# A two-block transformer kernel on one core: weights, activations and position bias laid out on the host in the order of their fetches

## The chip, the core and the metric

The kernel runs on one core of a Trainium2 chip. A core has a matrix engine (TensorE, PE in the rows; its weight loads are shown apart as PEld), a vector engine (VectorE, DVE), an engine for activation functions (ScalarE, ACT), a general one (GpSimd, POOL) and SyncE (SP), which here only issues loads and stores. Sixteen DMA engines move data between the chip's main memory (HBM) and the on-chip buffers that the engines compute on. Every engine works through its own instructions in a fixed order and waits on semaphores for the others.

The metric is the device time of one execution in microseconds (us).

## What is computed

256 rows of 1,024 numbers (float32) pass through four attention layers and two large feed-forward parts. The reference, cut to its frame:

```
x = even_layer(x, ...)                    # 8 products of rms_norm(x) with w_in, two kinds of attention, w_out
x = odd_layer(x, ...)                     # windowed attention with sinks; chunked attention with a bias by position
h = rms_norm_2(x, attn_norm[0]);  x = x + dsa_mixer(h, ...)         # top-k chosen keys
h = rms_norm_2(x, mlp_norm[0]);   x = x + squared_relu_mlp(h, mlp_w_up[0], mlp_w_down[0])
h = rms_norm_2(x, attn_norm[1]);  x = x + mla_mixer(h, ...)         # low-rank queries, keys, values
h = rms_norm_2(x, mlp_norm[1]);   x = x + squared_relu_mlp(h, mlp_w_up[1], mlp_w_down[1])
return rms_norm_2(x, final_norm)
```

The bias by position of the second layer is one number for each head and each distance between query and key:

```
rel = iq[:, None] - ik[None, :]
ridx = jnp.clip(rel, -(CHUNK - 1), REL_MAX) + (CHUNK - 1)     # 64 - 1, 256
s = s + rel_table[:, ridx]                                    # rel_table: 8 heads x 320
```

## The kernel before

**Products.** Activations lie with features on the 128 partitions (`xT`, 8 tiles of 128 features by 256 tokens). Every float32 operand is split into two reduced-precision halves, high and low (`h`, `l` for activations, `wh`, `wl` for weights), and a product is the sum of three matmuls (high by high, low by high, high by low). `N.tokens` gives a product with tokens on the partitions (matmuls of line 185), `N.features` one with features on the partitions (line 216).

**Weights.** Each product with a matrix of 1,024 rows is fed in blocks of 1,024 numbers a partition, 512 KB, as a rule four row tiles by 256 columns. `fetch` (line 115) issues one DMA on SP's queue for a block, into one of four buffers `raw`. ScalarE then copies it to `wh` (line 161), which rounds it, and VectorE subtracts to get `wl` (line 162). 24 matmuls use a block, and then the next block's buffer is due. In HBM a block is 512 pieces of 1 KB: each partition gets four pieces, a row tile apart, at a pitch of one row of the matrix (4,104 numbers, 16,416 bytes, for `even_w_in`; 4,096 numbers for `mlp_w_up`). The very first block is fetched in two halves between the loads of `x`.

**Order.** A list of names for each layer (`ORDER0` to `ORDER3`) gives the order in which the program is written, and a scheduler then sets the order on each engine from priorities; the queues themselves are in order. In layer 0 the list's first parts are the products for queries and keys, the statistics of the layer's norm (`layer_stats`: column sums on TensorE at line 325, then some ten short VectorE instructions from line 343 on), the head norm (lines 421 to 434), and the turning of queries and keys by TensorE (`split_t`, `split_k`: line 386). `forget_log` (`BL`) fetches a narrow block of eight columns (`narrow`, tile `wn`, lines 125 to 128).

**Waits of the loads.** A fetch may start when the buffer it fills has been read by VectorE (the `wl` of four blocks earlier), and SP issues nothing else while it waits. The tables of linear position bias (`alibi`, line 741) go through SP's queue too; the buffers `bias` (three) serve both kinds of bias.

**Bias by position.** `rel_bias` (lines 963 to 973) builds, for each of eight heads, a 128 by 384 table: two fills of a masked corner by GpSimd and four DMAs on GpSimd's queue, each of which reads 64 partitions that start one number apart in the 320 numbers of the head. The table is then stored mirrored, and the softmax reads it backwards (`falling=True`, line 521).

## Time and profile before

| | |
|---|---|
| median of 3 runs | 879.75 us (879.03 to 883.26) |
| the profiled execution's own time | 882.59 us |
| its span, first to last instruction | 880.9 us |
| TensorE busy | 846.0 us (96% of the span) |
| VectorE, ScalarE, GpSimd busy | 670.3, 578.8, 52.0 us |
| loads on SP's queue | 129,696 packets, 134.20 MB, 55.0% of the DMA engines' time |

Where TensorE is busy, it computes; what a change can win is to be looked for where it is idle or runs at a lower clock. Of the span's 40 slices of 22 us, the page shows TensorE under 90% in six: the first two, the seventh (132 to 154 us), the twelfth (242 to 264 us), the 28th and the last. The DMA engines are busiest in the first six, seven tenths or more in five of them. The share of DMA time and the GB/s are to be read together: a high share at few GB/s means packets that take long.

### The profile page before, as it was taken

Reading aid. Unit: us, or ns where it says so; the run is one execution under the profiler, and the core shown is the slowest. Engines: PE = TensorE matmul, PEld = TensorE weight load, DVE = VectorE, ACT = ScalarE, POOL = GpSimd, SP = SyncE. Lnnn points to the kernel's source line nnn. Section 1 sums busy time; section 2 is a strip of 40 time slices with the busy share of each in tenths; the row PEclk is TensorE's granted clock in tenths of the full one; section 3 lists DMA queues with packets and bytes.
Section 4 is the critical chain, followed back from the end, with each engine's and each line's share of the span. In section 5 each row is a group of like instructions: output and inputs, shape, how many; then the busy total and the mean of one; then the engine's idle time right before and its main releaser. Section 6 shows DMA issues by size and latency. Waiting matters only on the chain. (4 is left out here: it accounts for less than half of the span.)

```text
span 880.9 us, 17702 instructions
## 1 busy us (share of the span) xinstructions
PE 846.0 (96%) x6554; PEld 813.6 (92%) x6554; DVE 670.3 (76%) x1799; ACT 578.8 (66%) x1379; POOL 52.0 (6%) x130
## 2 busy tenths in 40 slices
PE   6899997999989999999999999998999999999996
PEld 6799987999989999899999999998999998889986
DVE  5879986789888879988765577668999966556654
ACT  5597974669787666987664466555997765446542
POOL 8100000002330100000000000002000000000000
PEclk9899998999999999999999999999999999999999
DMA  8979595554655652335655666553324665566751
GB/s 211 175 156 169 92 82 174 177 174 119 178 129 168 181 145 73 122 116 170 185 184 185 190 189 194 185 164 98 124 73 123 201 188 173 187 182 191 215 169 48
DMA packets 131430, 137.83 MB, mean 156 GB/s; under 512 B 8289, under 2 KB 123121, under 8 KB 131345
## 3 DMA queue, kind: packets, MB, share of 16 engines
q1 hardware_dynamic: 129696, 134.20, 55.0%
q0 software_dynamic: 1360, 1.99, 1.5%
q8 instruction: 51, 0.84, 0.4%
q10 hardware_dynamic: 288, 0.52, 0.2%
q14 instruction: 35, 0.28, 0.1%
HBM read 135.65 MB, written 1.05 MB: 155 GB/s over the span
## 5 line engine op out<-in xcount | busy, mean ns | idle before, releaser
L161 ACT ACTIVATE wh<-raw 128x512 fp32r<-128x512 f32 (+2 forms) x548 | 290.3, 571 | 221.3 <-issue 102.1
L162 DVE TENSOR_TENSOR wl<-raw,wh 128x512 fp32r<-128x512 f32 (+2 forms) x548 | 322.7, 620 | 126.7 <-ACT wh L161 119.9
L216 PE MATMUL mm<-ar,wh 128*128 128x256 f32 (+1 forms) x1664 | 304.8, 283 | 0.5 <-ACT ar L701 0.4
L216 PEld LDWEIGHTS mm<-ar,wh 128*128 128x128 f32 (+1 forms) x1664 | 258.0, 190 | 2.0 <-ACT ar L701 1.3
L185 PE MATMUL mm<-wh,ar 128*128 128x256 f32 (+2 forms) x1168 | 238.3, 299 | 9.0 <-ACT wh L161 7.5
L216 PE MATMUL mm<-ar,wl 128*128 128x256 f32 x832 | 234.4, 283 | 0.0
L185 PEld LDWEIGHTS mm<-wh,ar 128*128 128x128 f32 x1168 | 188.5, 192 | 14.5 <-ACT wh L161 7.8
L185 PE MATMUL mm<-wl,ar 128*128 128x256 f32 (+2 forms) x584 | 174.1, 299 | 1.1 <-DVE wl L162 1.1
L216 PEld LDWEIGHTS mm<-ar,wl 128*128 128x128 f32 x832 | 157.5, 190 | 0.4 <-DVE wl L162 0.2
L185 PEld LDWEIGHTS mm<-wl,ar 128*128 128x128 f32 x584 | 111.7, 191 | 4.4 <-DVE wl L162 2.0
L216 PE MATMUL s<-ar,wh 128*128 128x256 f32 x512 | 90.4, 279 | 0.0
L216 PEld LDWEIGHTS s<-ar,wh 128*128 128x128 f32 x512 | 78.0, 188 | 0.0
L216 PE MATMUL s<-ar,wl 128*128 128x256 f32 x256 | 71.4, 279 | 0.0
L524 ACT ACTIVATE se<-sx,mx 128x128 f32<-128x128 f32 (+1 forms) x128 | 57.1, 451 | 4.9 <-DVE mx L521 4.3
L216 PEld LDWEIGHTS s<-ar,wl 128*128 128x128 f32 x256 | 48.1, 188 | 0.0
L216 PE MATMUL pv<-ar,wh 128*128 128x256 f32 x256 | 45.1, 279 | 0.0
L216 PEld LDWEIGHTS pv<-ar,wh 128*128 128x128 f32 x256 | 39.0, 188 | 0.0
L216 PE MATMUL pv<-ar,wl 128*128 128x256 f32 x128 | 35.7, 279 | 0.0
L544 DVE TENSOR_TENSOR pt<-tp,pt 128x384 fp32r<-128x384 f32 x60 | 32.2, 552 | 3.4 <-ACT pt L543 2.9
L493 PE MATMUL s<-kbh,ar 128*128 128x512 f32 (+1 forms) x112 | 31.2, 354 | 0.8 <-ACT kbh L397 0.7
L543 ACT ACTIVATE pt<-tp 128x384 fp32r<-128x384 f32 x60 | 27.9, 486 | 1.1 <-PE tp L542 0.7
L1213 ACT ACTIVATE ar<-u 128x512 fp32r<-128x512 f32 x32 | 20.3, 633 | 11.8 <-DVE u L1211 11.7
(309 smaller groups left out, 1157.9 us busy)
## 6 DMA issues: line engine op xcount, KB each, us to landing
raw<-in_mlp_w_up SPq DMA_DIRECT2D x64, 512.0 KB, 3.8
raw<-in_mlp_w_down SPq DMA_DIRECT2D x64, 512.0 KB, 4.0
raw<-in_even_w_in SPq DMA_DIRECT2D x31, 512.0 KB, 9.1
raw<-in_odd_w_in SPq DMA_DIRECT2D x26, 512.0 KB, 4.7
raw<-in_a_w_in SPq DMA_DIRECT2D x16, 512.0 KB, 3.7
raw<-in_even_w_out SPq DMA_DIRECT2D x8, 512.0 KB, 4.6
raw<-in_odd_w_out SPq DMA_DIRECT2D x8, 512.0 KB, 3.4
raw<-in_a_w_out SPq DMA_DIRECT2D x8, 512.0 KB, 3.6
```

The lines of the kernel that those rows point to most:

```text
L161: nc.scalar.activation(hi[:, c:e], raw[:, c:e], AF.Copy)
L162: nc.vector.tensor_tensor(out=lo[:, c:e], in0=raw[:, c:e], in1=hi[:, c:e].bitcast(F32), op=OP.subtract)
L185: nc.tensor.matmul(view[t], lhsT=x[:, s], rhs=w[:, j, :], start=(k + j == 0 and i == 0 and (t == 0 or not one)), stop=(k + j == nkt - 1 an ...
L216: nc.tensor.matmul(acc[:width, m * T:(m + 1) * T], lhsT=w[:, j, m * P:m * P + width], rhs=x, start=(k + j == 0 and i == 0 and m == 0), sto ...
L493: nc.tensor.matmul(o, lhsT=a_[:, gq, qt * P:(qt + 1) * P], rhs=b_[:, gk, 0:n], start=(i == 0), stop=(i == 2 and last))
L524: nc.scalar.activation(e[:, c:c + n], x[:, c:c + n], AF.Exp, bias=m[:, i:i + 1], scale=-1.0, accum_out=z[:, i:i + 1])
L543: nc.scalar.activation(h, p[:, :W], AF.Copy)
L544: nc.vector.tensor_tensor(out=l, in0=p[:, :W], in1=h.bitcast(F32), op=OP.subtract)
L1213: nc.scalar.activation(h, u, AF.Copy)
```

## The change

The host now writes all weights into one array, block after block in the order in which the program issues its fetches, and each block as the buffer holds it: partition by partition, the partition's 1,024 numbers in one run (4 KB). `fetch` reads such a block as 128 runs and notes in a list what the block is (the plan), by which the host fills the array. Names of weights and row offsets take the place of the tensors (`Weight`). The sizes, the number and the order of the fetches as the program is written stay as they were. `x` is laid out so that a partition's two row tiles of one load lie side by side (2 KB in one run). The bias by position is expanded on the host to 8 tables of 128 by 384 and is fetched with one DMA a head, as rows of 1,536 bytes; it is stored in reading order, so the softmax reads it forwards, and the two fills and the three other DMAs are gone. The narrow block of eight columns is laid out as the others, 64 numbers a partition.

```diff
     def fetch(self, src, k0, nk, c0, nco, into=None):
         if into is None:
             into = self.fetched = self.stream.tile([P, 1024], F32, tag="raw", name=self.uid("raw"), bufs=RAW)
-        self.nc.sync.dma_start(out=into[:, :nk * nco].rearrange("p (k c) -> p k c", k=nk),
-                               in_=src[k0 * P:(k0 + nk) * P, c0:c0 + nco].rearrange("(k p) c -> p k c", p=P))
+        n = nk * nco
+        self.nc.sync.dma_start(out=into[:, :n], in_=bass.AP(tensor=self.weights.tensor,
+                                                            offset=self.weights.offset + self.placed,
+                                                            ap=[[n, P], [1, n]]))
+        self.plan.append((self.placed, src.name, src.layer, src.row + k0, nk, c0, nco))
+        self.placed += n * P
         return self.fetched
...
-    xr = a["x"].rearrange("(k p) t -> p k t", p=P)
+    xr = a["x"]
...
-                                           in1=like(b[:, ::-1] if falling else b, s[i]), scale=-1.0, scalar=BIG if init is None else init, op0=OP.add,
+                                           in1=like(b, s[i]), scale=-1.0, scalar=BIG if init is None else init, op0=OP.add,
...
     def rel_bias(h):
-
         b = N.tmp("bias", W)
-        nc.gpsimd.memset(b[0:64, 0:64], NEG)
-        nc.gpsimd.memset(b[0:64, 256:256 + 64], NEG)
-        for p0, c, n in ((0, 64, 192), (64, 0, 256), (0, 256 + 64, 64), (64, 256, 128)):
-            e0 = (p0 + 128 - 255 if c < 256 else p0 - 127) + (c % 256) + 63
-            nc.gpsimd.dma_start(out=b[p0:p0 + 64, c:c + n],
-                                in_=bass.AP(tensor=rt.tensor, offset=rt.offset + h * 320 + e0,
-                                            ap=[[1, 64], [1, n]]))
+        nc.gpsimd.dma_start(out=b, in_=a["relpos"][h])
         return b
...
-    z["x"] = np.ascontiguousarray(f["x"][0].T)
+    z["x"] = np.ascontiguousarray(f["x"][0].T.reshape(KT, P, T).transpose(1, 0, 2))
...
+def packed(inputs, plan, size):
+    z = np.empty(size, np.float32)
+    for at, name, layer, row, nk, c0, nco in plan:
+        block = np.asarray(inputs[name])[layer, row * P:(row + nk) * P, c0:c0 + nco]
+        z[at:at + nk * P * nco] = block.reshape(nk, P, nco).transpose(1, 0, 2).ravel()
+    return z.reshape(1, size)
```

In layer 0, in the layers after layer 1 and in both feed-forward parts the instructions of every engine stand in the same order as before. In layer 1 the shorter `rel_bias` moves some of them. On GpSimd, at the first head's table (`bias`), there stood before:

```order
L966 MEMSET bias_3315 64x64
L967 MEMSET bias_3315 64x64
L970 DMA bias_3315<-in_d_rel_bias 64x192
L970 DMA bias_3315<-in_d_rel_bias 64x256
L970 DMA bias_3315<-in_d_rel_bias 64x64
L970 DMA bias_3315<-in_d_rel_bias 64x128
L966 MEMSET bias_3322 64x64
```

and now, with the fills and pieces gone:

```order
L976 DMA bias_3315<-in_relpos 128x384
L976 DMA bias_3317<-in_relpos 128x384
L976 DMA bias_3441<-in_relpos 128x384
L976 DMA bias_3443<-in_relpos 128x384
L976 DMA bias_3671<-in_relpos 128x384
```

Eight issues now stand where 16 fills and 32 issues stood. On VectorE, at the first pair of these heads (`sx`, `mx`: scores with their bias and the row maximum, of one head and the other; `wl`: weight blocks being split; `ms`: the next head norm), there stood before:

```order
L534 TENSOR_SCALAR se_3049<-se_3049,rz_3058 128x256
L162 TENSOR_TENSOR wl_3240<-raw_3237,wh_3239 128x256 x3
L162 TENSOR_TENSOR wl_3276<-raw_3273,wh_3275 128x256 x3
L521 ISA sx_3339,mx_3338<-s_3329,bias_3315 128x256
L521 ISA mx_3338 128x1
L521 ISA sx_3339,mx_3338<-s_3330,bias_3315 128x128
L521 ISA mx_3338 128x1
L425 TENSOR_REDUCE ms_3064<-sq_3219 128x8
L521 ISA sx_3345,mx_3338<-s_3329,bias_3322 128x256
```

and now:

```order
L547 TENSOR_SCALAR se_3049<-se_3049,rz_3058 128x256
L534 ISA sx_3329,mx_3328<-s_3319,bias_3315 128x256
L534 ISA mx_3328 128x1
L534 ISA sx_3335,mx_3328<-s_3319,bias_3317 128x256
L534 ISA mx_3328 128x1
L177 TENSOR_TENSOR wl_3240<-raw_3237,wh_3239 128x256 x2
L534 ISA sx_3329,mx_3328<-s_3320,bias_3315 128x128
L534 ISA mx_3328 128x1
L534 ISA sx_3335,mx_3328<-s_3320,bias_3317 128x128
L534 ISA mx_3328 128x1
L177 TENSOR_TENSOR wl_3240<-raw_3237,wh_3239 128x256
L177 TENSOR_TENSOR wl_3276<-raw_3273,wh_3275 128x256 x2
```

The scores with bias now stand ahead of the six pieces of weights that they stood behind. On SP, in the same layer, two of the tables of linear bias (`bias` from `alibi`) have moved past a weight block each; before:

```order
L115 DMA raw_570_3394<-in_odd_w_in 128x4x256
L115 DMA raw_611_3567<-in_odd_w_in 128x4x256
L741 DMA bias_592_3507<-in_alibi 128x384
L115 DMA raw_614_3603<-in_odd_w_in 128x4x256
L115 DMA raw_649_3759<-in_odd_w_in 128x4x256
L115 DMA raw_652_3795<-in_odd_w_in 128x4x256
L741 DMA bias_593_3509<-in_alibi 128x384
```

and now:

```order
L127 DMA raw_570_3384<-in_weights 128x1024
L754 DMA bias_592_3487<-in_alibi 128x384
L127 DMA raw_611_3547<-in_weights 128x1024
L127 DMA raw_614_3583<-in_weights 128x1024
L127 DMA raw_649_3729<-in_weights 128x1024
L754 DMA bias_593_3489<-in_alibi 128x384
L127 DMA raw_652_3765<-in_weights 128x1024
```

Each table stands one block earlier, and the blocks `raw_611` and `raw_652` one table later.

## Rows read from the trace of the kernel before

**Rows 1.** The page, first part: busy time of the engines
```profile
PE 846.0 (96%) x6554; PEld 813.6 (92%) x6554; DVE 670.3 (76%) x1799; ACT 578.8 (66%) x1379; POOL 52.0 (6%) x130
```

**Rows 2.** Timeline of TensorE: start, duration, line, count [idle before, releaser]
```profile
6.11 0.80 PE L185 MATMUL mm<-wh,ar 128*128 128x256 f32 x2 [6.11 <-ACT wh L161]
...
22.10 0.50 PE L325 MATMUL tp<-ones,acc 128*128 128x2 f32 x4
...
34.94 1.12 PE L386 MATMUL tp<-ident,u 128*128 128x128 f32 x4 [4.34 <-DVE u L434]
...
50.17 0.38 PE L901 MATMUL tp<-upto,ar 128*128 128x256 f32 x1 [1.27 <-ACT ar L896]
...
138.64 0.69 PE L332 MATMUL tp<-ident,rs_y 128*128 128x128 f32 x2 [4.84 <-DVE pt L544]
...
244.65 1.23 PE L386 MATMUL tp<-ident,u 128*128 128x128 f32 x8 [2.21 <-DVE pt L544]
```

**Rows 3.** Stretches of TensorE: length, busy (matmuls), granted clock, DMA share, GB/s
```profile
9.46:13.00 3.54, 3.54 (x15) 1.00 1.07 329
14.00:22.00 8.00, 8.00 (x70) 1.00 0.97 183
36.00:40.50 4.50, 4.50 (x23) 0.50 1.02 72
...
128.30:133.80 5.50, 5.50 (x48) 1.00 1.00 89
139.40:143.70 4.30, 4.30 (x24) 0.57 0.33 96
...
245.90:249.50 3.60, 3.60 (x21) 0.59 0.88 233
```

**Rows 4.** Timeline of ScalarE, the waits for loads and one for TensorE
```profile
24.96 0.26 ACT L127 ACTIVATE wn<-raw 128x64 fp32r<-128x64 f32 x1 [0.71 <-DMA raw<-in_even_w_in]
...
128.35 1.16 ACT L161 ACTIVATE wh<-raw 128x512 fp32r<-128x512 f32 x2 [2.18 <-DMA raw<-in_even_w_in]
...
135.56 1.15 ACT L161 ACTIVATE wh<-raw 128x512 fp32r<-128x512 f32 x2 [4.51 <-DMA raw<-in_even_w_in]
...
233.89 1.34 ACT L161 ACTIVATE wh<-raw 128x256 fp32r<-128x256 f32 x4 [3.73 <-DMA raw<-in_odd_w_in]
...
249.41 0.38 ACT L337 ACTIVATE rfm<-tp 128x256 f32<-128x256 f32 x1 [1.63 <-PE tp L332]
```

**Rows 5.** Timeline of VectorE at the same places
```profile
26.39 0.15 DVE L343 TENSOR_SCALAR st_v<-tp 128x2 f32<-128x2 f32 x1
...
34.20 1.29 DVE L434 TENSOR_TENSOR u<-u,rs_y 128x512 f32<-128x512 f32 x2
...
41.17 0.17 DVE L684 COPY lf<-tp 128x16 f32<-128x16 f32 x1 [2.23 <-PE tp L679]
...
144.29 0.69 DVE L717 TENSOR_TENSOR u<-mm,rfm 128x512 f32<-128x512 f32 x1 [2.17 <-PE mm L216]
...
222.00 2.10 DVE L162 TENSOR_TENSOR wl<-raw,wh 128x256 fp32r<-128x256 f32 x6
```

**Rows 6.** Loads issued from 105 to 120 us, and from 250: KB each, median us to landing
```profile
raw<-in_even_w_in SPq DMA_DIRECT2D x4, 512.0 KB, 14.1
...
raw<-in_odd_w_out SPq DMA_DIRECT2D x7, 512.0 KB, 3.4
```

**Rows 7.** Stretches: busy PE, PEld, DVE, ACT, POOL (instructions), clock, DMA share, GB/s
```profile
51.10:58.00 6.90, 6.90 (x61) 6.90 (x60) 4.50 (x16) 6.78 (x19) 0.00 (x0) 1.00 0.48 106
60.00:80.00 20.00, 19.67 (x164) 19.24 (x163) 18.20 (x58) 15.49 (x31) 0.38 (x2) 1.00 1.03 148
```

**Rows 8.** Bias by position: GpSimd's DMAs; softmax reads, ns min/median/max, backwards and forwards
```profile
L970 POOL DMA_DIRECT2D bias<-in_d_rel_bias x32 | 16.7, 529 | 0.0
...
L521 DVE CUSTOM_DVE_ANT_0 sx<-s,bias x32: 271/342/426, 43.4 to 262.7; 128x256 f32<-128x256 f32 x16, 128x128 f32<-128x128 f32 x16
...
L521 DVE CUSTOM_DVE_ANT_0 sx<-s,tri x16: 276/342/424, 93.7 to 120.3; 128x256 f32<-128x256 f32 x8, 128x128 f32<-128x128 f32 x8
```

More of the change, by code (lines that the diff above doesn't have):

```diff
@@ L51, with __init__, below @@
           "LW5 LO3 LO4 LT5 LO5 LS6 LS7 LK3 LW6 LT6 LO6 LW7 LT7 LO7")
+class Weight:
+    def __init__(self, name, layer=0, row=0):
+        self.name, self.layer, self.row = name, layer, row
+    def below(self, k):
+        return Weight(self.name, self.layer, self.row + k)
 class Net:
-    def __init__(self, ctx, tc):
+    def __init__(self, ctx, tc, weights, plan):
+        self.weights, self.plan, self.placed = weights, plan, 0
         self.tc = tc
@@ L227, in forward @@
 @with_exitstack
-def forward(ctx: ExitStack, tc: tile.TileContext, a: dict, out: bass.AP):
+def forward(ctx: ExitStack, tc: tile.TileContext, a: dict, out: bass.AP, plan: list):
     nc = tc.nc
-    N = Net(ctx, tc)
+    N = Net(ctx, tc, a["weights"], plan)
     keep = N.keep
-    def flat(name):
-        return a[name].rearrange("a k c -> (a k) c")
+    flat = Weight
     ones2 = keep.tile([P, 2], F32, name="ones2")
@@ L513, in like, with softmax @@
         return x if len(s.shape) == 2 else x.rearrange("p (t c) -> p t c", t=s.shape[1])
-    def softmax(s, bias, m, z, init=None, falling=False):
+    def softmax(s, bias, m, z, init=None):
         x = N.tmp("sx", W)
@@ L599, in weigh_shared, with weights_of @@
         return acc
-    def weights_of(s, bias, sinks=None, falling=False):
+    def weights_of(s, bias, sinks=None):
         z = N.tiny("sz", 4)
@@ L605, in weights_of @@
         es = [softmax(s[n], bias[n], m[:, 2 * n:2 * n + 2], z[:, 2 * n:2 * n + 2],
-                      None if sinks is None else nsink[:, sinks[n]:sinks[n] + 1], falling) for n in range(2)]
+                      None if sinks is None else nsink[:, sinks[n]:sinks[n] + 1]) for n in range(2)]
         if sinks is not None:
@@ L1021, in rel_weights @@
         s = scores_pair(gd[b, "q"], gd[b, "k"], n, n)
-        gd["e", j] = weights_of(s, bias, falling=True)
+        gd["e", j] = weights_of(s, bias)
     def rel_turn(j):
@@ L1233, in forward @@
     for half in range(2):
-        hid = hidden(a["mlp_w_up_2"][0], half, None if half else after)
+        hid = hidden(Weight("mlp_w_up_2", 0), half, None if half else after)
         if half == 0:
@@ L1328, in lat_q @@
     def lat_q(b):
-        blocks = [(k, nk) + N.wload_as(wq[k * P:(k + nk) * P], nk, b * 384, 384, q_order) for k, nk in ((0, 2), (2, 1))]
+        blocks = [(k, nk) + N.wload_as(wq.below(k), nk, b * 384, 384, q_order) for k, nk in ((0, 2), (2, 1))]
         pq = N.tokens(latent("q"), None, 3, None, 384, blocks=blocks)
@@ L1388, in forward @@
     for half in range(2):
-        hid = hidden(a["mlp_w_up_2"][1], half, None if half else after)
+        hid = hidden(Weight("mlp_w_up_2", 1), half, None if half else after)
         if half == 0:
@@ L1471, in arrange @@
            for h in range(8)]).astype(np.float32)
-    return z
+    table = f["d_rel_bias"][0][:, np.clip(q - k, -63, 256) + 63]
+    z["relpos"] = np.where((behind >= 0)[None], table, np.float32(NEG)).astype(np.float32)
+    return z
+def packed(inputs, plan, size):
+    import numpy as np
+    z = np.empty(size, np.float32)
[3 more added lines that the diff above has]
+    return z.reshape(1, size)
 def kernel(**inputs):
@@ L1484 @@
         aps[n] = nc.dram_tensor(f"in_{n}", v.shape, mybir.dt.from_np(v.dtype), kind="ExternalInput").ap()
+    size = sum(inputs[n].size for n in _WEIGHTS)
+    aps["weights"] = nc.dram_tensor("in_weights", (1, size), F32, kind="ExternalInput").ap()
     out = nc.dram_tensor("out_0", (1, T, D), F32, kind="ExternalOutput").ap()
+    plan = []
     with tile.TileContext(nc) as tc:
-        forward(tc, aps, out)
+        forward(tc, aps, out, plan)
+    assert sum(nk * P * nco for _, _, _, _, nk, _, nco in plan) == size
+    arrays["in_weights"] = packed(inputs, plan, size)
     got = _run(nc, [arrays], core_ids=[0])
```

11 lines of the change are left out of this document (5 added, 6 removed).

## The prediction

> **What bounds the kernel now.** I read the page's busy times first. TensorE is busy for 846.0 of 880.9 us [rows 1], so a change to loads can win only where TensorE is idle or slow. Next I read the timeline of TensorE alone, looking for brackets with idle time. Three pauses above 2 us stand out: 4.34 us before 34.94, 4.84 us before 138.64 and 2.21 us before 244.65 [rows 2]. Third come stretches of TensorE around these pauses, with the granted clock. [...] In the first of them 23 matmuls take 4.5 us, 196 ns each, against 70 in 8 us, 114 ns, at full clock. A pause of 1.27 us before 50.17 [rows 2] is followed by a clock of 1.00 [rows 7]: a pause that short costs itself alone.
>
> Fourth I followed each pause back. The releaser is always VectorE, but what had held VectorE up is a load. At 128.35 and 135.56 ScalarE stands 2.18 and 4.51 us before a weight block that hasn't landed [rows 4]; VectorE's subtraction waits for ScalarE's copy, and the softmax piece that TensorE wants stands behind it in VectorE's queue. The four loads issued from 105 to 120 us take 14.1 us to land, against 3.4 for blocks of the same size later [rows 6]. While the DMA engines are busy for the whole of 128.3 to 133.8, they move 89 GB/s; elsewhere at full share 329 or 183 [rows 3]. So these loads are slow in their packets, and it isn't their number. Before 244.65 it is the same: ScalarE waited 3.73 us at 233.89 for a block [rows 4], while the four pieces a head of the position bias ran on the same DMA engines.
>
> The first pause is less direct. VectorE starts the norm's statistics (`st_v`) at 26.39, though TensorE had started the column sums for it at 22.10 [rows 2, 5]. Ahead of it in VectorE's queue stands the split of the narrow block, whose copy waited on its load until 24.96 [rows 4]. From 26.39 VectorE works nearly without a break to 34.20, where it scales the queries that TensorE's turning at 34.94 waits for.
>
> **The change, part by part.**
>
> *The fetches.* Their count, bytes and issue order in layer 0 stay, each block is now 128 runs of 4 KB in place of 512 of 1 KB. No row shows such a load. The nearest rows bound it: at worst the 14.1 us stay; at best it is the 3.4 us of the later blocks [rows 6]. (A sixth off the 14.1 us, 2.4 us a block, would already end the two waits of 2.18 and 4.51 us [rows 4], which are what is left over behind several such loads.) In rate: 72 to 183 GB/s as in the slow stretches, or 329 as in the stretch from 9.46 [rows 3]. Longer packets could also make another queue's small load wait longer; no pause was traced back to one, so the end below nothing is no more than a few tenths. I take the fast end, because `even_w_in` is the one matrix that shows the slow rates at length, and its pitch of 16,416 bytes is what sets it apart from the rest, and it disappears.
>
> [...] The rows show 72, 89, 183 and 329 GB/s at full share with the same 1 KB runs [rows 3]. [...]
>
> First term, the start. TensorE needs 96 matmuls before the column sums. The first begins at 6.11 [rows 2]; I leave that time, since the first load of `x` is too early to be queued behind much. It runs at half pace to about 13 (15 matmuls in 3.54 us from 9.46, though the clock's record says 1.00 there), then at 114 ns [rows 3]. Fed without gaps: 7 us at 236 ns are 30 matmuls, the other 66 take 7.5 us, so the sums come at 20.6, and `st_v` half a us later, at 21.2, not 26.39: 5.2 us. That asks that the narrow block has landed by 20; up to it 1 MB of `x`, six blocks of 512 KB and two tables are issued, some 4.6 MB, 14 us at 329 GB/s, so it can. VectorE's 7.8 us from `st_v` to the scaling stay, being work. TensorE has 65 matmuls meanwhile, 7.4 us from 21.2 to 28.6, and is wanted at 34.94 - 5.2 = 29.7: it pauses 1.1 us, less than the 1.27 that left the clock alone. **5.2 us.**
>
> Second term, the clock behind it. It's half from 34.94 to about 41, a loss of some 3 us; but VectorE can follow only as far as it waited for TensorE there, 2.23 us at 41.17 [rows 5]. **2.2 us.**
>
> Third term, 138.64. The pause of 4.84 us has its cause in the two waits for loads, 6.7 us together, so it goes whole. Behind it VectorE waits 2.17 us for a TensorE at half clock [rows 5], which is what the clock gives back. **7.0 us.**
>
> Fourth term, 244.65. The pause is 2.21 us, and ScalarE waits 1.63 us for TensorE behind it [rows 4]: 0 to 3.8 us. The order here is new, so I take the pause alone. **2.2 us.**
>
> *The position bias.* 32 issues of 529 ns [rows 8] become 8, on an engine busy for 52 us in all [rows 1]; nothing that TensorE waits for stands behind them but the tables, which come sooner. Bytes go from 160 to 192 KB a head. The read turned round costs VectorE nothing: the 32 reads of a stored bias, half of them backwards, have the same median, 342 ns, as the 16 forward ones of `tri` [rows 8]. Priced in the fourth term.
>
> *`x`.* Runs of 2 KB in place of 1 KB in four loads: inside the first term.
>
> *The rest.* Behind 245 us the timeline of TensorE shows no pause as long as that of 2.21 us, and none goes back to a late block. Faster loads there are hidden: I take 0, and grant 1 us.
>
> Sum: 5.2 + 2.2 + 7.0 + 2.2 = 16.6 us. From the profiled execution's 882.59 us that is 866.0; this execution is 2.8 us above the median of the runs shown, 879.75, and from the median it comes to **863**. With the upper bounds (all of the half clock, 3.8 at 244.65, a us of the rest) the gain is 20.5 us; with VectorE a little late at each place about 12.
>
> **The rivals.**
>
> *VectorE takes the wait over.* From 60 to 80 us VectorE is busy for 18.20 of 20 us, TensorE for 19.67 [rows 7]. If VectorE can't run ahead, the 7.4 us won at the start are given back by 100 us, and terms three and four stay: 9.2 us, time 870.5. For it: VectorE's small margin. Against it: in that stretch it is TensorE that has no margin at all.
>
> *The loads stay slow.* If the slow packets come from something that stays (other traffic on the memory, the place in memory and not the pitch), nothing moves: 879.75, with a us either way. For it: the stretch with 329 GB/s has blocks of `even_w_in` too, so the pitch alone doesn't always make them slow. Against it: a sixth off the landing time is enough for the third term, as said above.
>
> *More comes back.* The half pace of the start ends earlier because TensorE no longer pauses there, and all of the clock's loss returns: 22 us, time 857.5.
>
> *Slower, by the new order in layer 1.* The scores with bias now stand ahead of six pieces of weights, 2.10 us of VectorE's work [rows 5]. If their tables land late, VectorE waits there with the splits behind it; TensorE, which needs those, pauses for the 2.1 us and then loses about as much at half clock, as it did behind 244.65: some 4.5 us, so 884.3, if the loads bring nothing at the same time. It decides from a pause of about 2.2 us on [rows 2, 3], and only in the case of slow loads. Against it: one issue a table instead of four.
>
> **How the numbers follow.** What can be told from no change is about 0.5%, 4.4 us. Forecast, 863 (own range 858 to 868): 0.68. VectorE takes over, 870.5: 0.18. More, 857.5: 0.04. Loads stay slow, 879.75: 0.07. Slower, 884.3: 0.03. The first three are faster by over 0.5%: 0.90; then 0.07 and 0.03. The range of 856 to 873 holds the first three and leaves out the last two.
>
> **What would show it.** In the profile after: weight blocks of 512 KB landing in about 3 to 4 us everywhere, also from 105 to 120 us; ScalarE's waits for loads, as those of 2.18, 4.51 and 3.73 us [rows 4], nearly gone; `st_v` at about 21; the turning of the queries at about 30 after a pause near 1 us; no pause above 2 us at the later two places and clock 1.00 from there on. Wrong would be the prediction if the landing times stay above 8 us in the first 130 us, or if they fall and TensorE pauses as long before the same instructions.

## The result, and the profile after

The changed kernel takes 866.62 us (median of 4 runs, 865.52 to 868.05) against 879.42 us for the kernel before (4 runs, 879.03 to 883.26): a ratio of 0.9846, 95% interval 0.9814 to 0.9878. The gain is 12.8 us where 16.6 were forecast. The profiled execution took 868.05 us with a span of 866.4 us, 14.5 us less than the profiled execution before (882.59 and 880.9).

First the page of the kernel after: TensorE's busy time, and the packets, bytes and share of the DMA engines of SP's queue.

```profile
PE 840.8 (97%) x6554; PEld 808.7 (93%) x6554; DVE 670.6 (77%) x1799; ACT 577.7 (67%) x1379; POOL 40.7 (5%) x90
...
q1 hardware_dynamic: 39456, 134.20, 47.9%
```

The same bytes now travel in 39,456 packets where there were 129,696. The next view, the loads issued from 105 to 120 us (size, median us to landing), answers to [rows 6].

```profile
raw<-in_weights SPq DMA_DIRECT2D x4, 512.0 KB, 3.3
```

It was 14.1 us. So the first thing that the prediction asked to see is there. ScalarE's waits for weight blocks fall with it, from 14 waits of 23.8 us in all to 3 of 4.4, the longest 1.9 us. TensorE's timeline at the places of [rows 2], kernel after:

```profile
6.56 0.79 PE L200 MATMUL mm<-wh,ar 128*128 128x256 f32 x2 [6.56 <-ACT wh L176]
...
21.45 0.50 PE L338 MATMUL tp<-ones,acc 128*128 128x2 f32 x4
...
33.43 0.49 PE L399 MATMUL tp<-ident,u 128*128 128x128 f32 x2 [3.71 <-DVE u L447]
...
47.63 0.39 PE L914 MATMUL tp<-upto,ar 128*128 128x256 f32 x1 [1.27 <-ACT ar L909]
...
130.05 0.43 PE L345 MATMUL tp<-ident,rs_y 128*128 128x128 f32 x2
...
231.58 1.09 PE L399 MATMUL tp<-ident,u 128*128 128x128 f32 x8 [0.22 <-DVE pt L557]
```

Of the three pauses of [rows 2] the second (4.84 us before the two transposes, now at 130.05) is gone, the third (2.21 us) is down to 0.22, and the first is still 3.71 us. The stretches behind them (length, busy time of PE, PEld, DVE, ACT and POOL with instructions, granted clock, DMA share, GB/s):

```profile
33.43:37.50 4.07, 4.07 (x22) 4.07 (x23) 4.00 (x7) 2.33 (x5) 0.00 (x0) 0.58 0.41 142
100.00:120.00 20.00, 19.61 (x154) 18.74 (x153) 18.75 (x70) 19.40 (x58) 0.00 (x0) 1.00 0.37 131
120.00:140.00 20.00, 20.00 (x165) 19.47 (x164) 17.57 (x37) 13.20 (x28) 1.13 (x4) 1.00 0.46 159
232.00:236.00 4.00, 4.00 (x33) 3.63 (x32) 3.93 (x12) 3.87 (x11) 0.54 (x1) 1.00 0.58 193
```

The half clock is gone with the second and third pause (1.00 in the stretches behind both) and has stayed behind the first (0.58). Taking the same instructions in both traces shows where the 14.5 us were won; the last column adds up the terms of the prediction to the same place (at the turning 5.2, then the 2.2 behind it, at the spreading 4.84 of the third term's 7.0).

| place on TensorE | before, us | after, us | won so far | forecast so far |
|---|---|---|---|---|
| column sums | 22.10 | 21.45 | 0.65 | 1.5 |
| turning of the queries | 34.94 | 33.43 | 1.51 | 5.2 |
| sums of the forget gate | 50.17 | 47.63 | 2.54 | 7.4 |
| spreading of a norm (TensorE's two transposes of its factors) | 138.64 | 130.05 | 8.59 | 12.2 |
| turning in layer 1 | 244.65 | 231.58 | 13.07 | 16.6 |
| end of the span | 880.9 | 866.4 | 14.5 | 16.6 |

The start brought 2.5 of 7.4 us. Everything behind it brought 12.0 where 9.2 were forecast.

Why the start failed is in three other timelines. GpSimd's, kernel after:

```profile
10.03 6.66 POOL L861 COPY mine<-ident 32x8 f32<-32x8 f32 x4
16.63 0.71 POOL L865 DMA_DIRECT2D gm<-in_lams  x1
...
18.45 0.54 POOL L879 DMA_DIRECT2D nsink<-in_c_sinks  x1
...
20.76 0.95 POOL L140 MEMSET wn<- 128x1024 f32 x1
```

ScalarE's copy of the narrow block, and VectorE:

```profile
21.74 0.26 ACT L142 ACTIVATE wn<-raw 128x64 fp32r<-128x64 f32 x1 [2.57 <-POOL wn L140]
```

```profile
21.32 0.23 DVE L870 SCALAR_TENSOR_TENSOR lsc<-gm 128x64 f32<-128x64 f32 x1 [1.09 <-DMA gm<-in_lams]
...
23.92 0.24 DVE L882 COPY sink<-nsink 128x8 f32<-128x8 f32 x1 [2.37 <-DMA nsink<-in_c_sinks]
...
25.05 0.15 DVE L356 TENSOR_SCALAR st_v<-tp 128x2 f32<-128x2 f32 x1
...
32.69 1.28 DVE L447 TENSOR_TENSOR u<-u,rs_y 128x512 f32<-128x512 f32 x2
```

The tiles named here are small tables and constants: `mine` and `both` are cut out of the identity matrix `ident`; `gm` (128 KB on the chip), `nsink` and `fbias` (4 KB each), `pos_i` (1 KB) and `invf` (12 KB) are loads on GpSimd's queue. The narrow block's data are no longer late: ScalarE's copy waits for GpSimd's fill of its buffer, which stands behind four copies of 32 by 8 numbers that took 6.66 us. The loads of `gm` and `nsink` are issued by the same engine behind the same copies, and VectorE waits 1.09 and 2.37 us for them with `st_v` behind them in its queue. So `st_v` comes at 25.05 and not at 21.2, though the column sums were under way at 21.45.

**Theory.** (1) The loads were slow because of where the runs of `even_w_in` lie, and the new layout ends that. (2) The start is now held by GpSimd's queue: by the copies, and by the small loads behind them. **Rivals.** For (1): the length of the runs. For (2): VectorE and ScalarE have no margin in the start, so that moving GpSimd's work changes nothing; or one execution's chance.

### The profile page after: what moved, and what is told of

Same layout as the page of the kernel before. It is cut to its first block, busy times and chain, and to the rows that moved or that the text cites. A ratio compares the mean times of both kernels' runs of the same rounds, so it can differ in the third digit from the quotient of the medians.

```text
span 866.4 us, 17641 instructions
## 1 busy us (share of the span) xinstructions
PE 840.8 (97%) x6554; PEld 808.7 (93%) x6554; DVE 670.6 (77%) x1799; ACT 577.7 (67%) x1379; POOL 40.7 (5%) x90
## 3 DMA queue, kind: packets, MB, share of 16 engines
q1 hardware_dynamic: 39456, 134.20, 47.9%
q0 software_dynamic: 848, 2.25, 0.9%
## 5 line engine op out<-in xcount | busy, mean ns | idle before, releaser
L231 PE MATMUL mm<-ar,wh 128*128 128x256 f32 (+1 forms) x1664 | 301.0, 281 | 0.5 <-ACT ar L714 0.5
L231 PEld LDWEIGHTS mm<-ar,wh 128*128 128x128 f32 (+1 forms) x1664 | 255.0, 188 | 2.0 <-ACT ar L714 1.3
L537 ACT ACTIVATE se<-sx,mx 128x256 f32<-128x256 f32 (+1 forms) x128 | 57.2, 452 | 4.8 <-DVE mx L534 4.3
```

Source lines behind the costliest of these rows:

```text
L231: nc.tensor.matmul(acc[:width, m * T:(m + 1) * T], lhsT=w[:, j, m * P:m * P + width], rhs=x, start=(k + j == 0 and i == 0 and m == 0), sto ...
L537: nc.scalar.activation(e[:, c:c + n], x[:, c:c + n], AF.Exp, bias=m[:, i:i + 1], scale=-1.0, accum_out=z[:, i:i + 1])
```

## The experiments

The table gives ratios to the kernel before, which ran beside each of them on the same chip. Four chips were used; the medians of the kernel before there are 879.21 us (the weights alone, the bias alone, the copies moved, the three loads moved), 882.51 us (runs of 1 KB, 16,640 bytes, the five loads moved, with either `x`), 881.05 us (the angles put off, after once more) and 881.07 us (16,448 and 16,544 bytes).

| kernel | ratio | 95% interval |
|---|---|---|
| before, weight blocks alone packed | 0.9857 | 0.9830 to 0.9884 |
| before, bias by position alone by row | 0.9999 | 0.9987 to 1.0011 |
| after, blocks in runs of 1 KB | 0.9849 | 0.9825 to 0.9874 |
| before, `even_w_in` at a pitch of 16,640 bytes | 0.9877 | 0.9855 to 0.9898 |
| the same, 16,448 bytes | 0.9862 | 0.9832 to 0.9892 |
| the same, 16,544 bytes | 0.9865 | 0.9836 to 0.9893 |
| after, GpSimd's copies moved | 0.9832 | 0.9809 to 0.9856 |
| after, three small loads moved | 0.9845 | 0.9822 to 0.9869 |
| after, copies and five small loads moved | 0.9815 | 0.9795 to 0.9836 |
| that, and `x` as before | 0.9817 | 0.9797 to 0.9836 |
| copies and loads moved, and the angles put off | 0.9827 | 0.9808 to 0.9847 |
| after, once more | 0.9843 | 0.9817 to 0.9868 |

### Which part of the change?

**The weights alone.** The kernel after with `x` and the bias by position put back:

```
-    xr = a["x"]
+    xr = a["x"].rearrange("(k p) t -> p k t", p=P)
...
-        nc.gpsimd.dma_start(out=b, in_=a["relpos"][h])
+        (two fills and four DMAs a head, read backwards, as before)
```

> Before with the weight blocks alone laid out as they land; x and the relative-position bias as before. Theory: the third term (the pause at 138.64 and its half clock, 7.0 us) and the 1.5 us of the start come from the weights alone; the fourth place (2.21 us at 244.65) stays, if the bias pieces on GpSimd's queue are what slowed the block there: 2 to 4 us more than after, 868.5 to 870.5, ratio 0.987 to 0.990. Rival (the weights' layout does it all): the pause at 244.65 is under 0.5 us, the blocks there land in under 4.5 us, ratio 0.984 to 0.986.

Measured 867.54 us, 0.9857. The theory asked for 0.987 to 0.990 and the rival for 0.984 to 0.986; the interval reaches into both. The trace lies nearer to the rival, though that asked for a pause under 0.5 us and for blocks in under 4.5 us there: the pause is 0.67 us, and the blocks issued from 200 to 245 us landed in 4.7 us (5.4 in the kernel before, 4.6 in the kernel after). TensorE at the first and the last of the three places, and VectorE in the start:

```profile
32.34 1.11 PE L399 MATMUL tp<-ident,u 128*128 128x128 f32 x4 [3.65 <-DVE u L447]
...
230.83 1.09 PE L399 MATMUL tp<-ident,u 128*128 128x128 f32 x8 [0.67 <-DVE pt L557]
```

```profile
20.96 0.16 DVE L356 TENSOR_SCALAR st_v<-tp 128x2 f32<-128x2 f32 x1 [0.67 <-PE tp L338]
...
25.64 0.17 DVE L1056 CAST pos<-pos_i 128x2 f32<-128x2 int32 x1 [2.34 <-DMA pos_i<-in_positions]
...
31.60 1.29 DVE L447 TENSOR_TENSOR u<-u,rs_y 128x512 f32<-128x512 f32 x2
```

The last pause is 0.67 us though the bias pieces are the old ones. And the start says something new: here `st_v` came at 20.96, a shade before the forecast 21.2, and TensorE still paused 3.65 us. The 7.8 us from `st_v` to the scaling became 10.6; 2.34 us of it are a wait for `pos_i`, the positions, from which the angles of the rotary embedding are made; nothing in the start uses them. The lateness had moved on by one small load.

**The bias alone.** The kernel before with `rel_bias`, the tables and the softmax of the kernel after:

```
-        (two fills and four DMAs a head, read backwards)
+        nc.gpsimd.dma_start(out=b, in_=a["relpos"][h])
```

> Before with the relative-position bias alone stored by row. Theory (the pieces are part of the cause at 244.65): that pause falls from 2.21 to under 1 us, the two earlier ones (4.34 and 4.84 us) stay, 2 to 4 us faster: ratio 0.9955 to 0.998. Rival (the weights' layout alone decides): all three pauses stay, ratio 0.999 to 1.001.

Measured 879.58 us, 0.9999: the rival's figure, nothing that can be measured. TensorE at the second and third place:

```profile
138.12 0.43 PE L332 MATMUL tp<-ident,rs_y 128*128 128x128 f32 x2 [4.38 <-DVE pt L544]
...
242.34 1.09 PE L386 MATMUL tp<-ident,u 128*128 128x128 f32 x8 [1.38 <-DVE pt L544]
```

The third pause was 1.38 us in this execution, with clock 1.00 behind it (243 to 247 us). Neither theory said that: the pause is neither under 1 us nor what it was. In the kernels with the old bias and another pitch, below, it was 1.47, 2.12 and 1.78 us. It varies from run to run. But over all traces it falls into two groups that don't overlap: 1.38 to 2.21 us in the five with the weights in their old layout, and at most 1.09 us in the nine with packed weights, among them the one with the old bias (0.67 us). So its shortening goes with the packed weights; what the bias adds can't be told from these runs.

### What in the layout?

**Runs of 1 KB, blocks in one piece.** The kernel after, with each block still in one stretch of memory, but row tile by row tile:

```
-                                                            ap=[[n, P], [1, n]]))
+                                                            ap=[[nco, P], [P * nco, nk], [1, nco]]))
...
-        z[at:at + nk * P * nco] = block.reshape(nk, P, nco).transpose(1, 0, 2).ravel()
+        z[at:at + nk * P * nco] = block.ravel()
```

> The kernel after with every block still one stretch of memory in the order of its fetch, but inside it by rows of its (at most 4) row blocks, so that a partition gets runs of 1 KB as before and not one of 4 KB. Theory of place (what was slow is where the runs of `even_w_in` lie, by its pitch of 16,416 bytes, not their length): blocks land in 3 to 4.5 us everywhere, the pauses at 138.64 and 244.65 stay away, ratio 0.983 to 0.988. Theory of length (1 KB runs are slow by themselves when the queue is full): blocks take 8 to 14 us around 110 us, the pause before the softmax comes back with over 3 us, ratio above 0.993.

**Another pitch, and nothing else.** The kernel before with one line more; 56, 8 or 32 columns are added to the 4,104 and never read:

```
+    z["even_w_in"] = np.pad(f["even_w_in"], ((0, 0), (0, 0), (0, 56)))
```

> The kernel before with one edit: `even_w_in` is stored with 4160 columns instead of 4104, that is with rows that start every 16,640 bytes, a multiple of 256, instead of 16,416; the last 56 columns are never read. Theory (pitch): its blocks land in 3 to 5 us also from 105 to 120 us, the pause of 4.84 us at 138.64 is gone with its half clock: 7 us or more faster, ratio 0.983 to 0.992. Rival (which columns are fetched, not where their rows start): the fetches of the columns from 768, 1792, 2816 and 3840 still take 10 us or more and the ratio is 0.997 to 1.002.

> The kernel before with `even_w_in` stored with 4112 columns: rows every 16,448 bytes, a multiple of 64 but not of 256, so three of four rows start off a 256-byte boundary (the last 8 columns are never read). Theory A (a row that starts off 256 bytes is slow): between before and the kernel with 16,640 bytes, with three quarters of the rows off instead of seven eighths nearly as slow as before, ratio 0.995 to 1.000 and the blocks at 105 to 120 us still above 10 us. Theory B (rows that start off 64 bytes are slow): as fast as with 16,640 bytes, ratio 0.986 to 0.990, blocks in 3 to 4.5 us. Theory C (not alignment, but this one pitch of 16,416): as B.

> The kernel before with `even_w_in` stored with 4136 columns: rows every 16,544 bytes, an odd multiple of 32 as 16,416 is, so that rows start off 64 and off 256 bytes as often as before, in another order (the last 32 columns are never read). Theory A and theory B (alignment): the blocks at 105 to 120 us take 10 us or more, the pause of over 4 us at 138 stays, ratio 0.996 to 1.002. Theory C (the one pitch, by which the rows of a fetch fall on few places of the memory): blocks in 3 to 5 us, that pause gone, ratio 0.985 to 0.991.

Loads issued from 105 to 120 us in these four, in the order: runs of 1 KB in packed blocks, then pitch 16,640, 16,448 and 16,544:

```profile
raw<-in_weights SPq DMA_DIRECT2D x4, 512.0 KB, 3.9
```

```profile
raw<-in_even_w_in SPq DMA_DIRECT2D x3, 512.0 KB, 3.9
```

```profile
raw<-in_even_w_in SPq DMA_DIRECT2D x3, 512.0 KB, 4.0
```

```profile
raw<-in_even_w_in SPq DMA_DIRECT2D x3, 512.0 KB, 3.9
```

All four land in about 4 us where it took 14.1 [rows 6], and all four ratios lie from 0.985 to 0.988 beside 0.9846 of the whole change. So the first pitch's rival, that certain columns are slow to fetch, falls: they are still fetched. The length of the runs isn't it either: 1 KB does as well in the time, with 3.9 against 3.3 us a block. Nor is it alignment, which theories A and B of the last two runs wanted: at 16,544 bytes the rows start off 64 and off 256 bytes as often as at 16,416. Theory C holds in what it forecast, this one pitch; its reason (rows that fall on few places of the memory) is not shown. TensorE at the second place with 16,544 bytes:

```profile
130.92 0.43 PE L332 MATMUL tp<-ident,rs_y 128*128 128x128 f32 x2
```

There is no pause, from 32 columns that nobody reads. Why 16,416 is slow and its neighbours are not stays open: no run looked at the memory itself. Nor is the pitch slow everywhere: in the kernel before, single 512 KB blocks of `even_w_in` landed in anything from 4.6 us (issued from 97 to 100 us) to 16.5 (from 118 to 121). And more columns also make the matrix larger, so that other arrays may lie elsewhere; no run separates this from the pitch, though the bias-alone kernel, whose inputs differ too, kept the slow loads (14.7 us).

### What holds the start?

**The copies moved.** In the kernel after, the six small copies are written right behind `ident`, so that they run at about 2 us; the order on VectorE and ScalarE is unchanged.

```
+    both = ...; mine = ...        # fill and copies moved here, behind ident
     def g(base, i):
...
-    both = ...; mine = ...        # from their places in layer 0
```

> The kernel after, with GpSimd's six small copies (`mine`, `both`) written right behind `ident`, so that they run at about 2 us, when VectorE has little to do; all orders on VectorE and ScalarE stay. Theory (the start is now held by GpSimd: its copies stretch to 6.7 us beside VectorE's dense work, and the small loads and the memset of `wn` stand behind them): the four `mine` copies take about 1.8 us, the lams issue comes at 11 to 12 instead of 16.6, the `wn` memset at about 16 instead of 20.8, VectorE's waits of 1.09 and 2.37 us for the small loads go, `st_v` at 21.5 to 22 instead of 25.05, the turning at 30 to 30.5 instead of 33.43 with a pause under 1.3 us instead of 3.71, clock 1.00 from 20 to 40; 3 us and another 1 to 2 of half clock less than after: ratio to before 0.979 to 0.981, 861 to 863. Rival (VectorE and ScalarE have no margin at the start): `st_v` moves by under 1 us or the turning stays above 32.5, and the ratio stays at 0.984 to 0.986.

GpSimd, VectorE and TensorE:

```profile
2.84 0.89 POOL L280 COPY mine<-ident 32x8 f32<-32x8 f32 x4
...
19.59 0.72 POOL L1046 DMA_DIRECT2D pos_i<-in_positions  x1
```

```profile
21.67 0.16 DVE L364 TENSOR_SCALAR st_v<-tp 128x2 f32<-128x2 f32 x1 [0.26 <-PE tp L346]
...
24.95 0.17 DVE L1048 CAST pos<-pos_i 128x2 f32<-128x2 int32 x1 [0.93 <-DMA pos_i<-in_positions]
```

```profile
31.65 0.66 PE L407 MATMUL tp<-ident,u 128*128 128x128 f32 x4 [2.25 <-DVE u L455]
```

865.60 us, 0.9832. The copies take 0.89 us, `st_v` comes at 21.67 as the theory said. The fill of `wn` came at 18.39 and not at 16, since it waits 4.16 us for a buffer that TensorE has to release. The turning is at 31.65, not at 30 to 30.5: `pos_i` is issued behind that fill, and VectorE waits for it. So the theory held for `st_v` and the clock, which is 1.00 from 32 to 38 us, and missed the turning, the pause (2.25 us, not under 1.3) and the ratio (0.979 to 0.981).

**Three small loads moved.** `gm`, `nsink` and `fbias` are issued at 7.75 us, ahead of the copies, which stay:

```
+    lam4 = ...; nsink = ...; fbias = ...        # tiles and dma_start
     def turned(u, np_, n):
```

> The kernel after, with the issues of the three small loads (lams, nsink, fbias) in GpSimd's queue moved ahead of `cmask`, `tri` and the copies, to about 7.8 us; the copies stay where they are. Theory: the copies still take 5 to 7 us, so the `wn` memset stays at about 20.8; VectorE's waits for gm and nsink go, but the narrow block is now what holds it: wn at 22, `st_v` at 22.5 to 23, the turning at 31 to 31.5, pause 1.3 to 1.8; ratio to before 0.980 to 0.983, a us behind the kernel with the copies moved. Rival (no margin on VectorE): the turning stays above 32.5 and the ratio is 0.984 to 0.986. A second rival (the stretch of the copies is not caused by VectorE's density but by what stands ahead): the copies take about 2 us and the memset comes at 16.

```profile
11.58 2.40 POOL L871 COPY mine<-ident 32x8 f32<-32x8 f32 x4
```

```profile
32.81 0.66 PE L409 MATMUL tp<-ident,u 128*128 128x128 f32 x4 [2.65 <-DVE u L457]
```

866.41 us, 0.9845: no change in the time. The copies took 2.40 us here, so the second rival was right about them, though not about the fill of `wn`, which came at 19.15 and not at 16. The figures of the first rival came true (a turning above 32.5, 0.984 to 0.986), its reason did not: `st_v` was at 22.42, and VectorE then waited 1.33 us for `pos_i`.

**Copies and all five small loads moved**, and the same with `x` in its old layout.

```
+    lam4 = ...; nsink = ...; fbias = ...; pos_i = ...; invf = ...    # tiles and dma_start, at 9 to 12 us
     def turned(u, np_, n):
```

> The kernel after with GpSimd's copies written behind `ident` and all five of its small loads (lams, nsink, fbias, pos_i, invf) issued at about 9 to 12 us. Theory (behind the statistics VectorE's queue waits for the next small load, pos_i, as it did for 0.93 us with the copies alone moved and for 2.34 us where the weights alone were packed): no wait of VectorE for a small load is left, `st_v` at 21.5 to 22, the scaling of the queries 7.5 to 8.5 us behind it instead of 9.2, the turning at 30 to 30.8 with a pause under 1.3 us, clock 1.00; profiled span 861 to 862.5, ratio 0.979 to 0.983. Rival (what stands between `st_v` and the scaling is VectorE's and ScalarE's work alone): the 9.2 us stay and the turning is at 31.3 or later, ratio 0.983 to 0.985.

> As the kernel with the copies and the five small loads moved, and x laid out as before (runs of 1 KB). Theory (x in 2 KB runs made the first load land later, ScalarE's first copy at 5.08 instead of 4.18): the first matmul comes 0.4 to 0.8 us sooner, at about 5.8 instead of 6.4, and the column sums with it; ratio 0.978 to 0.982. Rival (the first load's time is chance): the first matmul within 0.2 us of the kernel with x packed, the ratio the same within 0.001.

VectorE and TensorE of the first of the two:

```profile
23.58 0.15 DVE L364 TENSOR_SCALAR st_v<-tp 128x2 f32<-128x2 f32 x1
...
30.22 1.29 DVE L470 TENSOR_TENSOR u<-u,rs_y 128x512 f32<-128x512 f32 x2
```

```profile
30.96 0.66 PE L422 MATMUL tp<-ident,u 128*128 128x128 f32 x4 [2.21 <-DVE u L470]
```

866.49 us and 865.86 us, 0.9815 and 0.9817. VectorE waits for no load any more, and the scaling follows `st_v` by 6.6 us. But `st_v` is late again, at 23.58: with their loads early, the instructions for the angles now stand ahead of it. The turning is at 30.96, the pause 2.21 us with half clock behind it (0.56 from 32 to 35 us), and the span 864.9 us; the theory had asked for a pause under 1.3 us, clock 1.00 and 861 to 862.5. The first row of `x` comes sooner in its old layout, as the theory said (the first matmul is at 5.91 us, in the kernel after at 6.56), but TensorE gives it back at once:

```profile
5.91 0.79 PE L200 MATMUL mm<-wh,ar 128*128 128x256 f32 x2 [5.91 <-ACT wh L176]
...
8.62 0.58 PE L200 MATMUL mm<-wh,ar 128*128 128x256 f32 x1 [0.76 <-ACT wh L176]
```

The column sums came at 21.34 with the old `x` and 21.18 with the new: in this pair its layout moves nothing. Over all the kernels with quick blocks they come at 20.95 to 21.89 us with the new `x`, and at 20.42, 20.72, 20.80, 21.34 and 22.75 with the old; whether the new layout costs the start some tenths stays open.

**The angles put off.** As the first of these two, and `pos` is made to depend on layer 1's statistics, so that the angles leave the start:

```
     nc.vector.tensor_copy(pos, pos_i)
+    nc.vector.scalar_tensor_tensor(out=pos, in0=c1, scalar=0.0, in1=pos, op0=OP.mult, op1=OP.add)
```

> As the kernel with the copies and all five small loads moved, and the angles of the rotary embedding (some 14 small VectorE instructions and a sine on ScalarE, first used behind layer 1) hung on layer 1's statistics by adding 0 times them to `pos`, so that none of them stands in the start. Theory (with the loads out of the way, what is left between the column sums and the turning is VectorE's own queue, to which the angles add about 2.5 us): `st_v` at 21.5 to 22, the scaling at 28 to 29, the turning at 28.7 to 29.8 without a pause above 0.5 us and with clock 1.00; span 2 to 3 us below the 864.9 of the kernel with the loads moved, less what the angles cost in layer 1; ratio 0.977 to 0.981. Rival (the turning is held by something else, TensorE's own queue or ScalarE): turning at 30.5 or later, ratio 0.981 to 0.983. Slower, if the angles and the two table loads of the sine land on layer 1's path: a new pause of 2 us or more between 140 and 200 us, ratio 0.982 or above.

VectorE and TensorE:

```profile
22.19 0.15 DVE L364 TENSOR_SCALAR st_v<-tp 128x2 f32<-128x2 f32 x1
...
28.75 1.29 DVE L470 TENSOR_TENSOR u<-u,rs_y 128x512 f32<-128x512 f32 x2
```

```profile
29.50 0.66 PE L422 MATMUL tp<-ident,u 128*128 128x128 f32 x4 [1.02 <-DVE u L470]
```

865.48 us (865.22 to 865.83), 0.9827. The turning and the pause are those that the prediction worked out: 29.5 (29.7 forecast), 1.02 us (1.1 forecast), clock 1.00 behind it. That is in part luck: `st_v` is 1.0 us later than the forecast 21.2, and the scaling follows it by 6.56 us in place of 7.8, since the angles, which were part of the 7.8, are gone. The run's own theory asked for a pause under 0.5 us and 0.977 to 0.981; both were missed. Part of the gain is given back in layer 1: the angles stand at 172 to 178 us now, and TensorE pauses for 0.65 and 0.36 us at 190 and 193 us, where the kernels with the copies moved show none and 0.17. That the angles make these pauses is argued, not shown.

**The kernel after once more.**

> The kernel after once more, on the chip and beside the runs of before that the kernel with the angles moved has: ratio 0.983 to 0.987; by the theory 1 to 1.5 us of the difference to the kernels with the copies and loads moved is in the pause at 33.4 and the clock behind it, so this one should be the slower by 0.3 to 0.8%. The rival (one execution's chance: the copy of 5.5 us and the late small loads of the shown profile do not come back): `mine` under 3 us and `st_v` before 22 in its profile.

GpSimd, VectorE and TensorE:

```profile
10.24 1.51 POOL L861 COPY mine<-ident 32x8 f32<-32x8 f32 x4
```

```profile
22.34 0.16 DVE L356 TENSOR_SCALAR st_v<-tp 128x2 f32<-128x2 f32 x1 [0.67 <-PE tp L338]
```

```profile
31.63 0.66 PE L399 MATMUL tp<-ident,u 128*128 128x128 f32 x4 [1.56 <-DVE u L447]
```

867.35 us (863.96 to 868.40), 0.9843. The rival was half right: in this execution of the same kernel the four copies took 1.51 us and not 6.66, `st_v` came at 22.34 and not before 22, and the pause was 1.56 us with clock 1.00 behind it. The ratio is in the theory's 0.983 to 0.987, but this kernel is slower than those with the copies and loads moved by 0.1 to 0.3% and not 0.3 to 0.8. The sums of the forget gate came at 44.42 instead of 47.63, so that the start brought 5.75 of the forecast 7.4 us here. The spreading of the norm and the turning in layer 1:

```profile
126.80 0.43 PE L345 MATMUL tp<-ident,rs_y 128*128 128x128 f32 x2
...
229.41 1.09 PE L399 MATMUL tp<-ident,u 128*128 128x128 f32 x8 [1.09 <-DVE pt L557]
```

They stood at 130.05 and 231.58. So the 6.66 us are chance: of nine profiled executions with the copies at 9.4 to 10.3 us, two show 6.66 us and seven 1.51 to 1.78. The other of the two is the kernel with runs of 1 KB, where VectorE waits 1.48 and 2.59 us for `gm` and `nsink` and TensorE pauses 4.52 us before the turning. The two executions of this kernel differ by 3.25 us at the norm and by 2.2 us in all (868.05 against 865.86 us). Beside this one the kernel with the copies moved has won nothing: turning 31.65 against 31.63, forget gate 44.40 against 44.42, norm 126.76 against 126.80. The kernel with the angles put off has no copies there, and its four runs lie within 0.6 us, where the five of this one spread over 4.4; but the other three with the copies moved spread over 1.2 to 2.9 us, and that the copies make the spread is not shown.

What is left when the copies take their usual time is `pos_i`. In the seven traces with quick blocks in which neither `gm` nor `nsink` is late and the angles stand where they did, `st_v` starts 0.53 or 0.54 us behind the column sums, and the scaling follows by 8.3 us and the wait for `pos_i`:

| kernel | VectorE's wait for `pos_i`, us | `st_v` to scaling, us |
|---|---|---|
| after, once more | 0.25 | 8.55 |
| after, copies moved | 0.93 | 9.24 |
| before, 16,448 bytes | 1.31 | 9.62 |
| after, three small loads moved | 1.33 | 9.65 |
| before, 16,544 bytes | 1.95 | 10.25 |
| before, weights alone packed | 2.34 | 10.64 |
| before, 16,640 bytes | 2.93 | 11.20 |

So of theory (2) the small load is shown, and the copies only for the executions in which they took 6.66 us. The 8.3 us themselves are nearly all VectorE's own work, as the first rival has it.

None of these versions is separated from the kernel after by its interval. By their ratios the best (0.9815 to 0.9832) would be worth another 1 to 3 us; but the lowest two stand beside the highest median of the kernel before, 882.51 us, and in us (866.49 and 865.86) they are hardly below the 866.62 of the kernel after.

## Why the prediction was right, and where it was wrong

The time, 866.62, lies in the range (856 to 873) and in the forecast's own (858 to 868), 3.6 us above the 863 forecast.

**Right: the loads, and why.** The choice of the fast end for the fetches rested on the pitch of 16,416 bytes. That is now shown, but for the size that goes with it: another pitch alone takes the pause of 4.84 us away and brings 0.986 to 0.988. Whether rows start on a multiple of 256 bytes plays no part that these runs show: a block took 3.9 us where all do (16,640 bytes), and 4.0 and 3.9 where three quarters and seven eighths don't (16,448 and 16,544).

**Right: term three, 7.0 us.** The pause is gone with its half clock (0.57 before, now 1.00). From the forget gate's sums to the turning in layer 1, less the shorter pause there, the traces differ by 13.07 - 2.54 - (2.21 - 0.22) = 8.5 us. The pause and what it had cost the clock are in it; 6.05 us had come by the place itself, where the pause was 4.84, so some 1.2 us are small waits that weren't listed (TensorE is idle for 6.38 us from the forget gate's sums to the place before, and for 0.43 after).

**Wrong: term one, 5.2 us, and with it term two, 2.2 us, in the first profiled execution.** They measured 2.5 us together there, and 5.75 us in the kernel after once more: 3.31 for term one and 2.44 for term two. The loads on SP's queue did come in time, as the first term asks ("That asks that the narrow block has landed by 20"), and `st_v` does stand half a us behind the column sums in the seven traces of the table above. What failed are two sentences. One is "VectorE's 7.8 us from `st_v` to the scaling stay, being work": they became 8.3 us (why not 7.8 stays open) and a wait for `pos_i` of 0.25 to 2.93 us. The other let small loads pass: "no pause was traced back to one, so the end below nothing is no more than a few tenths". Its reason there, longer packets, isn't what happened: `pos_i` took 5.8 us to land before as well. But there VectorE reached `pos_i` at 28.18, so that no wait showed; in the seven traces it gets there 2.6 to 4.9 us sooner, and the small load, which takes 4.6 to 7.3 us to land there, is not in time. In the first execution after, chance came on top: with the copies at 6.66 us, `gm` and `nsink` were late by 1.09 and 2.37 us, `st_v` came 3.9 us later than forecast, the pause was 3.71 us and the clock fell to 0.58, which is also close to the prediction's own sign of being wrong, a pause as long as before (4.34 us). Besides, in both executions the column sums come later than the forecast 20.6, at 21.45 and 21.80, because the first matmul starts at 6.56 and 6.50 and not at 6.11, and 14.9 and 15.3 us pass from it to the sums, not 14.5.

A turning that is sooner by 2 us isn't a gain of 2 us either: with the angles put off it came 2.13 us before that of the kernel after once more, but TensorE's pause was shorter by only 0.54 us (1.02 against 1.56): 0.66 us of the 2.13 stand already at the column sums, and for the other 0.93 TensorE did other matmuls meanwhile. At the spreading of the norm 1.00 us is left (125.80 against 126.80).

**Right in size, in part by luck: term four, 2.2 us (0 to 3.8).** It measured (2.21 - 0.22) + (14.5 - 13.07) = 3.4 us between the two profiles. In the second execution after the pause is 1.09 us and not 0.22, so that only 1.12 us of the pause are gone there. The bias, which shares this term, moved nothing in the time when it was changed alone; the packed weights go with the shorter pause, as shown above. And the half clock that the prediction saw behind it (0.59) is that of one execution: four other traces with the old layout of the weights show pauses of 1.38 to 2.12 us there with clock 1.00 behind them. The execution of before that was profiled was 3.2 us above its median of 879.42, that of after 1.4 above its own, which is the difference between 14.5 us in the profiles and 12.8 in the medians; that a part of the 3.4 us belongs to that execution is an estimate from this.

The prediction's upper bound, 20.5 us, isn't the sum of the parts that it names, which come to some 20.0 (3 us for the half clock of the start, 3.8 and 1 for the last two); the forecast of 863 doesn't depend on it.

**The rivals.** "VectorE takes the wait over" (870.5) came nearest, but not by its mechanism: what was won at the start wasn't given back by 100 us (the 2.54 us at the forget gate are still in the 8.59 at the norm), and from 60 to 80 us TensorE is busy for 19.96 of 20 us. The wait was taken over by a small load on GpSimd's queue, which no rival named; the prediction mentions it and prices it at a few tenths. "The loads stay slow" and "slower, by the new order in layer 1" are refuted by the landings and by the pause of 0.22 us at 231.58 (1.09 us in the second execution).

## What to carry to other kernels

When a long wait goes, list everything that stands in the waiting engine's queue ahead of the instruction you count on, each with its own releaser, and ask of each when it would be ready without the wait; here small loads and a fill on GpSimd's queue had hidden in the shadow of a big wait. If one matrix loads several times slower than others of the same run length, try a few unused columns before a new layout: here that alone had some eight to nine tenths of the gain by its ratio. And look at two executions before explaining a pause: two of the same program, one with four GpSimd copies stretched to 6.66 us, lay 2.2 us apart, and a fix for the copies had nothing to win in the usual one.

## What the runs showed of the hardware that was not expected

- Rows at a pitch of 16,416 bytes, read in runs of 1 KB, made the 512 KB blocks issued from 105 to 120 us land in 14.1 us (14.7 in a second kernel with that layout); at 16,448, 16,544 and 16,640 bytes it is 3.9 to 4.0 us. Over all 31 such blocks of the matrix the median is 9.1 us before, and 4.0 to 4.4 at the other pitches.
- Four GpSimd copies of 32 by 8 numbers took 0.89 to 0.91 us where they ran at 2.8 us, ahead of the matmuls and the splits of the weights. Behind 9 us they took 1.51 to 2.40 us, and twice 6.66. The two copies of 32 by 32 behind them took 0.82 to 1.13 us in eight traces, 3.15 us in that of the kernel before and 5.10 us at a pitch of 16,544 bytes. What stretches them is not shown.
- Loads of 1 to 12 KB on GpSimd's queue took 3.0 to 7.7 us from issue to landing in the start (7.3 us for the 1 KB of `pos_i` at a pitch of 16,640 bytes).
- Equal pauses left the clock in different states. The stretch from 32 to 35 us (columns as above) in the kernel with copies and loads moved, and in that with `x` as before, each behind a pause of 2.21 us:

```profile
32.00:35.00 3.00, 3.00 (x18) 3.00 (x17) 3.00 (x6) 2.95 (x7) 0.00 (x0) 0.56 0.34 79
```

```profile
32.00:35.00 3.00, 3.00 (x28) 3.00 (x27) 3.00 (x6) 2.98 (x6) 0.00 (x0) 1.00 0.29 76
```

  Once 18 matmuls at half clock, once 28 at full. Behind 2.65 us (three small loads moved) the clock was 1.00 as well. So a pause of this length decides nothing by itself, and the half clock behind it is no sure term of a sum.
